# Sample attention of a decoder layer: both pages of a pair scored in one TensorE run, with two turned-page buffers and one raw-weight buffer

## The chip, the cores and the metric

The kernel runs on one core of one Trainium2 chip. The metric is the device time of one execution in microseconds (us); three executions of the kernel before were timed.

## The reference

One layer of a decoder runs for two groups that share all parameters: a prompt group (1 sequence of 2048 tokens) and a sample group (8 sequences of 4 new tokens each, with 8192 past tokens in a paged cache). What bears on the change:

```python
h = rms_norm(x, pre_g)
z = h @ w_in                     # 1024 -> 5632: ca cb cg | pu pg | q k v sg | mq mg, 512 columns each
mk, mv = split(rms_norm(mem_prompt, mem_g) @ w_mem_kv)      # 256 memory tokens, 1024 columns
# stick-breaking attention of the sample group: 8 heads x 64, 64 pages of 128 tokens per sequence
k_past = cache_k[0][page_table]; v_past = cache_v[0][page_table]
zs = q @ k^T / 8 + bias_h
beta, 1 - beta = sigmoid(zs), sigmoid(-zs)
a_j = beta_j * prod over later tokens (1 - beta)            # a suffix product over the keys
y_s = a @ v
# then: gates, concat of four branches -> w_out -> rms_norm -> residual, final rms_norm
```

All data are float32. The products with `w_in` and `w_mem_kv` are made from three products of reduced-precision parts: each weight and each activation is split into a high part and the rest (`whi`, `wlo`, `xhi`, `xlo`).

## The kernel before

TensorE's instructions stand in the order in which the program writes them; the other engines' instructions, and the DMAs on SyncE's queue (SP), are ordered by a list scheduler at build time, which works from its own estimates. Each engine then runs its list strictly in order.

**The projection stage** takes the first 1502 us. It runs over two parts of the prompt (1024 tokens each; the first part also has the 32 sample tokens) and, in each part, over 44 column blocks of `w_in` of 128 columns ("kinds": q0, q1, ..., sg3). A block is computed in column tiles of the tokens, three in the first part (384, 384 and 288 tokens) and two in the second (512 each), with 24 matmuls per tile (`mm3`, line 242). Most groups hold one block; some hold two, whose tiles alternate. While the blocks q2, q3 and k0 of the first part run, one of eight blocks of `w_mem_kv` (m0 to m7, 24 matmuls of 256 tokens) stands between each two of their tiles.

**Weights.** A block's weights arrive as one raw tile of 512 KB (`load_w`, line 226, tag `wr`, on SP's queue). ScalarE casts it to `whi` (line 232), then GpSimd subtracts to get `wlo` (line 233). There are two buffers each of `whi` and `wlo`, and `WR` raw buffers (2). `fill_w` is called whenever a block has been used up: it splits the next raw tile and orders the load of another. A raw buffer is free for its next load once GpSimd's subtraction has read it. The blocks are taken in the order of `SEQ_W`: q0, q1, q2, m0, m1, m2, q3, m3, m4, m5, k0, m6, m7, k1, k2, ...

**The sample group's attention** (`sample_stages`) is slipped in between the matmuls of this stage: a counter of projection work (`due`) lets the generator take one step about every 5 us. The eight sequences are taken four at a time; the 64 pages of such a four are taken in 32 pairs, from the last to the first, so there are 64 pairs in all. For one pair n:
- `load_k(n, ml)`, `load_v(n)`: GpSimd issues indirect DMAs (line 892): two of 1 MB for the two pages' keys (`kt`, KT = 2 buffers), four of 512 KB for the values (`vt`, VB = 4 buffers).
- `turn(n, ml)`: VectorE transposes a page of keys in 32 x 32 blocks into `T` (line 925, two instructions per page, TB = 1 buffer), then the next pair's load into the freed `kt` is ordered.
- `scores(n, ml)`: 16 matmuls of 32 stationary columns in four column groups of the array (line 938, two records each in the trace) into one PSUM bank (`sSA`).
- `weights(n)`: two sigmoids on ScalarE (`sgam`, `sbe`, lines 949 and 951), the suffix product on VectorE (a scan, line 955) and a product (line 958).
- `transposes(n)`: two full-array transposes on TensorE (line 965), copied out by ScalarE (`saT`, line 967).
- `values(n)`: 8 matmuls of 32 stationary columns and 512 moving columns (line 977, two records each).

The order per pair, with `yield` as the step to the projection matmuls:

```python
for n in range(N):
    yield
    scores(n, 0); turn(n, 1)
    yield
    if n: transposes(n - 1); yield
    scores(n, 1)
    if n: values(n - 1); load_v(n)
    weights(n)
    turn(n + 1, 0)
    yield
```

So between two stretches of projection matmuls TensorE does, in turn: one page of scores; two transposes; one page of scores and the values of the pair before. After the projection stage come the prompt's stick-breaking attention and the output projection (1502 us to the end), which share nothing with the change.

Of the kernel before, what the change touches and what calls it, by code (L numbers as in the profile page):

```python
# [8 lines left out]
F32 = mybir.dt.float32  # L9
# [9 lines left out]
P = 128  # L19
# [13 lines left out]
PART = 1024  # L33
COLS = (((0, 384), (384, 768), (768, 1056)), ((0, 512), (512, 1024)))
XW = 1056
TB = 1
SMALL = 4
K4 = 4
PACE = 4.0
# [14 lines left out]
VB = 4  # L54
# [4 lines left out]
SEND = 0.97  # L59
XA = 3  # L60
KT = 2
WR = 2


class Tasks:
# [21 lines left out]
def kernel(  # L87
# [9 lines left out]
    pe, act, dve, pool, sp = nc.tensor, nc.scalar, nc.vector, nc.gpsimd, nc.sync  # L97
# [151 lines left out]
    st = zx.enter_context(tc.tile_pool(name="st", bufs=2, side="left"))  # L249
    tasks = Tasks()  # L250

    def big(name, bufs=BIG):
        return st.tile([P, 1088], F32, tag="big", name=name, bufs=bufs)

    def small(name):
        return st.tile([P, 512], F32, tag="small", name=name, bufs=SMALL)
# [488 lines left out]
    def fill_w(n=2):  # L745

        while len(wsplit) < n and (raw or SEQ_W):
# [3 lines left out]
            wsplit[it] = split_w(raw.pop(it), "%d%s%d" % it)  # L751
        while n == 2 and len(raw) < WR and SEQ_W:
            next_raw()
# [53 lines left out]
    def sample_setup(sm, S):  # L807

        ptb = sm.tile([P, NB, NPAGE], I32, tag="T", name="ptb", bufs=TB)
        sp.dma_start(ptb.rearrange("p b n -> p (b n)"), page_table.rearrange("b n -> (b n)").partition_broadcast(P))  # L810
        io = sm.tile([P, 3], I32, name="io", bufs=1)
        pool.iota(io, pattern=[[0, 3]], base=0, channel_multiplier=1)
        iof = sm.tile([P, 3], F32, name="iof", bufs=1)
        dve.tensor_copy(iof, io)
        for c, w in ((0, 32), (1, 64)):
            for k in range(P // w):
                pr = slice(w * k, w * k + w)
                dve.tensor_scalar(out=iof[pr, c : c + 1], in0=iof[pr, c : c + 1], scalar1=-float(w * k), scalar2=None,
                                  op0=ALU.add)
        idk = sm.tile([P, 2, NPAGE], I32, name="idk", bufs=1)  # L820
        idv = sm.tile([P, NB, NPAGE // 2], I32, name="idv", bufs=1)
        for i in range(4):
            pr = slice(32 * i, 32 * i + 32)
            dve.tensor_scalar(out=idk[pr], in0=ptb[pr, i::4, :], scalar1=32.0, scalar2=iof[pr, 0:1], op0=ALU.mult,
                              op1=ALU.add)
        for k in range(2):
            pr = slice(64 * k, 64 * k + 64)
            dve.tensor_scalar(out=idv[pr], in0=ptb[pr, :, k::2], scalar1=64.0, scalar2=iof[pr, 1:2], op0=ALU.mult,
                              op1=ALU.add)
        S["idk"], S["idv"] = idk, idv  # L830

        b1 = sm.tile([P, 1], F32, name="b1", bufs=1)
        nb1 = sm.tile([P, 1], F32, name="nb1", bufs=1)
        e8 = sm.tile([P, P], F32, tag="vt", name="e8", bufs=VB)[:NH]
        bcol = sm.tile([NH, 1], F32, name="bcol", bufs=1)
        sp.dma_start(bcol, sb_bias.rearrange("o h -> h o"))
        pool.memset(e8, 0.0)
        ev = e8.rearrange("h (g x r) -> h g x r", g=4, x=2)
        pool.affine_select(out=ev, in_=ev, compare_op=ALU.not_equal, fill=1.0, base=0, pattern=[[-1, 4], [-4, 2], [0, 16]],
                           channel_multiplier=1)  # L840
        yield
        yield
        bp = tp_tile("bps")
        pe.matmul(bp[:, 0:1], lhsT=e8, rhs=bcol, start=True, stop=True)
        dve.tensor_copy(b1, bp[:, 0:1])
        dve.tensor_scalar(out=nb1, in0=b1, scalar1=-1.0, scalar2=None, op0=ALU.mult)
        S["b1"], S["nb1"] = b1, nb1

        rep = sm.tile([P, 4, 4, 32], F32, tag="vt", name="rep", bufs=VB)
        for jl in range(4):  # L850
            dve.tensor_copy(rep[:, jl], ident[:, None, 32 * jl : 32 * jl + 32].to_broadcast([P, 4, 32]))
        yield
        qps = tp_tile("qps")
        for j in range(16):
            pe.matmul(qps[:, NS * j : NS * (j + 1)], lhsT=rep[:, j % 4].rearrange("p i d -> p (i d)"),
                      rhs=qsT[:, j // 4, :], start=True, stop=True)
        qv = qps.rearrange("p (r j t) -> p r j t", r=2, j=8)
        S["W"] = []
        for k in range(2):
            W = sm.tile([P, 2, 8, 2, TS, 4], F32, name=f"W{k}", bufs=1)  # L860
            pool.memset(W, 0.0)
            for i in range(4):
                pr = slice(32 * i, 32 * i + 32)
                t0 = TS * (4 * k + i)
                for r in range(2):
                    dve.tensor_copy(W[pr, r, :, r, :, i], qv[pr, r, :, t0 : t0 + TS])
            S["W"].append(W.rearrange("p r j x q i -> p (r j) (x q i)"))

        h8 = sm.tile([P, 4, 2, 4], F32, name="h8x", bufs=1)
        pool.memset(h8, 1.0)  # L870
        pool.affine_select(out=h8, in_=h8, compare_op=ALU.is_ge, fill=0.0, base=0, pattern=[[-32, 4], [-4, 2], [-8, 4]],
                           channel_multiplier=1)
        pool.affine_select(out=h8, in_=h8, compare_op=ALU.is_ge, fill=0.0, base=3, pattern=[[32, 4], [4, 2], [8, 4]],
                           channel_multiplier=-1)
        H8 = sm.tile([P, 2, 4], F32, name="H8", bufs=1)
        dve.tensor_tensor(out=H8, in0=h8[:, 0], in1=h8[:, 1], op=ALU.add)
        for i in (2, 3):
            dve.tensor_tensor(out=H8, in0=H8, in1=h8[:, i], op=ALU.add)
        S["H8"] = H8
        S["gam"] = []  # L880
        for k in range(2):
            g = sm.tile([P, 257], F32, name=f"sgam{k}", bufs=1)
            pool.memset(g[:, 256:257], 1.0)
            S["gam"].append(g)
        S["Oc"] = con.tile([P, 2, DH], F32, name="Oc")
        yield

# [6 lines left out]
    def sample_stages(sm, sps, S):  # L894
# [25 lines left out]
        def turn(n, ml):  # L920
            if n < N:
                T = sm.tile([P, 4, 16, 32], F32, tag="T", name=f"T{n}_{ml}", bufs=TB)
                kt = kts.pop((n, ml))
                for hh in range(2):
                    dve.transpose(T[:, 2 * hh : 2 * hh + 2].rearrange("p s j t -> p (s j t)"),  # L925
                                  kt[:, 2 * hh : 2 * hh + 2].rearrange("p s j d -> p (s j d)"))
                Ts[n, ml] = T
                load_k(n + 1, ml)
# [12 lines left out]

        def weights(n):
            sS = sSs.pop(n)
            be = sm.tile([P, 256], F32, tag="sbe", name=f"sbe{n}", bufs=2)
            ga = S["gam"][n % 2]

            tok = sS[:, :256].rearrange("p (m s t) -> p m t s", m=2, s=4)
            by = dict(m=2, s=4)
            act.activation(out=ga[:, 0:256].rearrange("p (m t s) -> p m t s", **by), in_=tok, func=AF.Sigmoid,
                           bias=S["nb1"][:, 0:1], scale=-1.0)  # L950
            act.activation(out=be.rearrange("p (m t s) -> p m t s", **by), in_=tok, func=AF.Sigmoid,
                           bias=S["b1"][:, 0:1])
            E = sm.tile([P, 257], F32, tag="sE", name=f"sE{n}", bufs=2)
            prev = S.get("E") if n % NCK else None
            dve.tensor_tensor_scan(out=E[:, ::-1], data0=ga[:, ::-1], data1=zeros.to_broadcast([P, 257]),
                                   initial=1.0 if prev is None else prev[:, 0:1], op0=ALU.mult, op1=ALU.max)
            S["E"] = E
            dve.tensor_tensor(out=be, in0=be, in1=E[:, 1:257], op=ALU.mult)
            As[n] = be

        def transposes(n):
            aps = S["ps"][:, 256:512]
            bs = As.pop(n).rearrange("p (k s) -> p s k", s=2)
            for k in range(2):
                pe.transpose(aps[:, P * k : P * (k + 1)], bs[:, k, :], ident)
            aT = sm.tile([P, 2, P], F32, tag="saT", name=f"saT{n}", bufs=2)
            act.copy(aT.rearrange("p l r -> p (l r)"), aps)
            aTs[n] = aT.rearrange("p l (x i) -> p l x i", i=4)

# [21 lines left out]
        for _ in range(Y0):  # L991
            yield
        turn(0, 0)
        for n in range(N):
            yield
            scores(n, 0)
            turn(n, 1)
            yield
            if n:
                transposes(n - 1)  # L1000
                yield

            scores(n, 1)
            if n:
                values(n - 1)
                load_v(n)
            weights(n)
            turn(n + 1, 0)
            yield
        yield  # L1010
        yield
        yield
# [764 lines left out]
    S = {}  # L1777
# [222 lines left out]
    for n, x in enumerate(parts):  # L2000
# [14 lines left out]
        for k, p_ in enumerate(out_part(x) if n >= len(lead_) else lead if not n else ()):  # L2015
# [5 lines left out]
            if not n:  # L2021

                k, at_ = p_ % 4, p_ // 4
# [41 lines left out]
```

## Time and profile before

| | |
|---|---|
| median of three executions | 2429.65 us (2429.42 to 2430.13) |
| profiled execution, first to last instruction | 2426.4 us |
| TensorE busy | 2290.7 us, 94% |
| VectorE, ScalarE, GpSimd busy | 72%, 46%, 52% |
| mean granted TensorE clock | 0.982 |
| DMA | 562 MB, 231 GB/s of HBM traffic over the span |

The profile is of one execution, and its own time is its span of 2426.4 us; the timed median is 3.25 us (0.13%) above it. Lines of a timeline give start, duration, engine, line and operation, output<-input, count, and in brackets the idle time before with what ended it. "PEld" is TensorE's weight load, "SPq" the issue of a DMA by SyncE.

### The profile page before, as it was taken

To read this page: it belongs to the slowest core of one execution; us is meant where nothing else is said; L and a number is where in the kernel's file an instruction comes from. 1 tells how busy PE (TensorE), PEld (TensorE's weight loads), DVE (VectorE), ACT (ScalarE), POOL (GpSimd) and SP (SyncE) were. 2 spreads that over 40 slices of the span, in tenths; PEclk is the share of its full clock that TensorE was granted. 3 is DMA by queue.
4 is the path that set the end of the run, shared out by engine and by line. 5 is a ranking of instruction groups with operands and counts; after the bars stand their busy time and mean duration, and the time that the engine had idled before them with its cause. 6 is when DMAs were issued, how large, how long until landed. Compare 5 with 4: busy or idle time off the path is not lost. (4 is left out here: it accounts for less than half of the span.)

```text
span 2426.4 us, 42151 instructions
## 1 busy us (share of the span) xinstructions
PE 2290.7 (94%) x15962; PEld 1776.1 (73%) x15962; DVE 1736.2 (72%) x2434; ACT 1118.5 (46%) x1939; POOL 1272.7 (52%) x1309
## 2 busy tenths in 40 slices
PE   6999999999999999999999999899999998989997
PEld 6998888898887777777777776455555556777775
DVE  5332784969756665477877877888898857886898
ACT  5322343242442322124241425688989955543444
POOL 2554545556574455655555554576876844433330
PEclk9999999999999999999999999999999999999998
DMA  5678988887778799987877776834332227887764
GB/s 184 213 253 285 350 290 292 290 263 265 261 253 275 271 346 329 312 285 253 290 265 271 260 239 164 239 81 118 101 88 73 63 63 239 272 279 254 238 240 161
DMA packets 340438, 562.15 MB, mean 232 GB/s; under 512 B 28481, under 2 KB 212929, under 8 KB 323834
## 3 DMA queue, kind: packets, MB, share of 16 engines
q1 hardware_dynamic: 284858, 290.72, 39.1%
q0 software_dynamic: 55376, 268.72, 31.1%
q8 instruction: 126, 2.06, 0.3%
q14 instruction: 78, 0.64, 0.1%
HBM read 469.28 MB, written 90.68 MB: 231 GB/s over the span
## 5 line engine op out<-in xcount | busy, mean ns | idle before, releaser
L925 DVE STREAM_TRANSPOSE T<-kt 128x1024 f32<-128x1024 f32 x256 | 308.8, 1226 | 193.6 <-PE sSA L938 183.0
L892 POOL DMA_INDIRECT vt<-in_cache_v_dram,idv x256 | 250.4, 978 | 239.7 <-PE sO L977 178.8
L583 DVE SCALAR_TENSOR_TENSOR cacc<-U,par,cacc 128x512 f32<-128x512 f32 x480 | 360.1, 750 | 11.8
L1277 POOL TENSOR_TENSOR be<-be,E 128x512 f32<-128x512 f32 (+2 forms) x320 | 303.5, 956 | 117.0 <-DVE E L1268 52.6
L1268 DVE TENSOR_TENSOR_SCAN E<-gam,cr,ZM 128x513 f32<-128x513 f32 x192 | 232.9, 1262 | 14.4 <-ACT gam L1253 13.2
L892 POOL DMA_INDIRECT kt<-in_cache_k_dram,idk x128 | 125.6, 981 | 206.9 <-DVE T L925 152.5
L1288 PEld LDWEIGHTS AT<-ident,be 128*128 128x128 f32 x1088 | 117.9, 142 | 127.3 <-ACT at L1294 45.3
L1885 PE MATMUL acc<-wohi,mh 128*128 128x512 f32 (+1 forms) x480 | 193.6, 403 | 3.9 <-DVE mh L1650 2.0
L1253 ACT ACTIVATE gam<-S,nbias_bc 128x1024 f32<-128x1024 f32 (+1 forms) x160 | 172.5, 1078 | 51.2 <-ACT be L1255 18.9
L1885 PE MATMUL acc<-wolo,mh 128*128 128x512 f32 (+1 forms) x480 | 190.8, 397 | 0.0
L1885 PE MATMUL acc<-wohi,ml 128*128 128x512 f32 x448 | 179.2, 400 | 12.1 <-DVE ml L1650 12.1
L1248 PE MATMUL S<-kT,Q 128*128 128x512 f32 (+1 forms) x640 | 177.9, 401 | 6.1 <-ACT be L1255 2.6
L1288 PE MATMUL AT<-ident,be 128*128 128x128 f32 x1088 | 158.4, 284 | 13.8 <-DVE at L1292 3.9
L1255 ACT ACTIVATE be<-S,bias_bc 128x1024 f32<-128x1024 f32 (+1 forms) x160 | 171.4, 1071 | 0.0
L1304 PE MATMUL av<-at,V 128*64 128x512 f32 (+3 forms) x640 | 153.0, 557 | 1.7 <-DVE sbo L1309 1.7
L938 PE MATMUL sSA<-T,W 128*32 128x128 f32 x4096 | 140.8, 277 | 7.6 <-DVE T L925 6.4
L938 PEld LDWEIGHTS sSA<-T,W 128*32 128x32 f32 x4096 | 105.4, 110 | 44.9 <-issue 37.2
L977 PE MATMUL sO<-vt,saT 128*32 128x512 f32 x1024 | 123.7, 597 | 0.0
L1248 PEld LDWEIGHTS S<-kT,Q 128*128 128x128 f32 x640 | 107.3, 196 | 22.2 <-ACT be L1255 3.5
L1650 DVE TENSOR_TENSOR ml<-mr,mh 128x512 fp32r<-128x512 f32 x108 | 97.0, 905 | 33.6 <-ACT mh L1639 33.4
L1265 DVE TENSOR_TENSOR_SCAN E<-gam,ZM 128x128 f32<-128x128 f32 (+3 forms) x128 | 96.4, 802 | 29.3 <-ACT gam L1253 22.3
L1294 ACT COPY at<-AT 128x512 f32<-128x512 f32 x192 | 109.0, 656 | 14.4 <-PE AT L1288 14.4
(571 smaller groups left out, 6032.8 us busy)
## 6 DMA issues: line engine op xcount, KB each, us to landing
Q<-qd SPq DMA_DIRECT2D x64, 256.0 KB
mr<-mixd SPq DMA_DIRECT2D x32, 512.0 KB
mr<-mixd SPq DMA_DIRECT2D x48, 256.0 KB
wor<-in_w_out_dram SPq DMA_DIRECT2D x20, 512.0 KB
xtp<-in_x_prompt_dram SPq DMA_DIRECT2D x16, 512.0 KB
kT<-kd SPq DMA_DIRECT2D x64, 128.0 KB
wor<-in_w_out_dram SPq DMA_DIRECT2D x32, 256.0 KB
msd<-mr SPq DMA_DIRECT2D x32, 256.0 KB
```

The lines of the kernel that those rows point to most:

```text
L583: dve.scalar_tensor_tensor(out=ps, in0=U[:, a + k : a + k + H], scalar=wd[:, k : k + 1], in1=ps, op0=ALU.mult, op1=ALU.add)
L892: pool.indirect_dma_start(out=dst, out_offset=None, in_=rows, in_offset=bass.IndirectOffsetOnAxis(ap=idx, axis=0))
L925: dve.transpose(T[:, 2 * hh : 2 * hh + 2].rearrange("p s j t -> p (s j t)"), kt[:, 2 * hh : 2 * hh + 2].rearrange("p s j d -> p (s j d)"))
L938: pe.matmul(sSs[n][32 * g : 32 * g + 32, P * ml : P * (ml + 1)], lhsT=W[:, jj, :], rhs=T[:, :, jj, :], start=i == 0, stop=i == 3, tile_pos ...
L1248: pe.matmul(S[:, j, :w], lhsT=Q[hh][:, x, P * (q2 + j) : P * (q2 + j + 1)], rhs=KT[hp, hh, kc][:, :w], start=x == 0, stop=x == 1)
L1253: act.activation(out=ga[:, :, 512 - w : 512], in_=S[:, :, :w], func=AF.Sigmoid, bias=nbias_bc[:, h : h + 1], scale=-1.0)
L1255: act.activation(out=be[:, :, :w], in_=S[:, :, :w], func=AF.Sigmoid, bias=bias_bc[:, h : h + 1])
L1268: dve.tensor_tensor_scan(out=E[:, j][:, ::-1], data0=ga[:, j][:, ::-1], data1=ZM[:, 0:1].to_broadcast([P, 513]), initial=carry[hh, q2][:, ...
L1277: pool.tensor_tensor(out=be[:, j, :m], in0=be[:, j, :m], in1=E[:, j, 513 - w : 513 - w + m], op=ALU.mult)
L1288: pe.transpose(ap_[:, P * qt : P * (qt + 1)], A[hp, qb, kc, hh, qt][:, P * r : P * (r + 1)], ident)
L1304: pe.matmul(av[64 * hh : 64 * hh + 64, c], lhsT=V[:, 4 * kc + r, 64 * hh : 64 * hh + 64], rhs=ats.pop((hp, qb, kc, r, hh))[:, c], start=dg ...
L1885: pe.matmul(o[:rows], lhsT=m[a][:, k, :rows], rhs=W[prod, 4 * h + k][w], start=not cont and h == k == n == 0, stop=h == 1 and k == 3 and n ...
```

## The change

`scores(n, 0)` moves from its own step down to the step of `scores(n, 1)`, so that both pages' scores and `values(n - 1)` stand in one run on TensorE; the step that it leaves is kept as an empty one, so that a pair still takes four steps. Both pages of the next pair are turned right after that run, into two `T` buffers instead of one. `transposes(n - 1)` comes two steps after `weights(n - 1)` instead of three, and two steps ahead of `values(n - 1)` instead of one. To make room in SBUF there is one raw-weight buffer instead of two (`WR`), and one buffer instead of two for `sgam`, `sbe` and `saT`; `h8x` uses a `vt` buffer during set-up, and the tag `big` is 32 columns narrower.

```diff
-TB = 1
+TB = 2
...
-WR = 2
+WR = 1
...
-        return st.tile([P, 1088], F32, tag="big", name=name, bufs=bufs)
+        return st.tile([P, 1056], F32, tag="big", name=name, bufs=bufs)
...
-        h8 = sm.tile([P, 4, 2, 4], F32, name="h8x", bufs=1)
+        h8 = sm.tile([P, 4, 2, 4], F32, tag="vt", name="h8x", bufs=VB)
...
-            be = sm.tile([P, 256], F32, tag="sbe", name=f"sbe{n}", bufs=2)
-            ga = S["gam"][n % 2]
+            be = sm.tile([P, 256], F32, tag="sbe", name=f"sbe{n}", bufs=1)
+            ga = S["gam"][0]
...
-            aT = sm.tile([P, 2, P], F32, tag="saT", name=f"saT{n}", bufs=2)
+            aT = sm.tile([P, 2, P], F32, tag="saT", name=f"saT{n}", bufs=1)
...
         turn(0, 0)
+        turn(0, 1)
         for n in range(N):
             yield
-            scores(n, 0)
-            turn(n, 1)
             yield
             if n:
                 transposes(n - 1)
                 yield
-
+                yield
+            scores(n, 0)
             scores(n, 1)
             if n:
                 values(n - 1)
                 load_v(n)
             weights(n)
             turn(n + 1, 0)
-            yield
+            turn(n + 1, 1)
```

In the instruction order of the changed program TensorE has 63 runs of page, page, values, one of two pages, one of values and 64 of transposes, where the program before has 65 runs of a page alone, 63 of page and values, one of values and 64 of transposes; TensorE's instructions are as many as before. On SP every load of a raw weight tile from the second on stands behind a wait for GpSimd's subtraction of the tile before it.

More of the change, by code (lines that the diff above doesn't have):

```diff
@@ L880, in sample_setup @@
         S["gam"] = []
[L881 to L884, printed above, removed]
+        g = sm.tile([P, 257], F32, name="sgam", bufs=1)
+        pool.memset(g[:, 256:257], 1.0)
+        S["gam"].append(g)
         S["Oc"] = con.tile([P, 2, DH], F32, name="Oc")
```

## The prediction

> **What bounds the kernel now.** I read the page first, then busy time by stretches of the span, then TensorE's waits in the projection stage, and then timelines around single runs of the sample group.
>
> ```profile
> span 2426.4 us, 42151 instructions
> ```
>
> ```profile
> core 0: us, PE busy (x) PEld busy (x) DVE busy (x) ACT busy (x) POOL busy (x), PEclk, DMA share, GB/s
> 0.00:56.00 56.00, 35.90 (x208) 32.51 (x209) 31.15 (x49) 30.60 (x63) 10.94 (x35) 1.00 0.59 197
> 56.00:126.00 70.00, 66.12 (x477) 64.03 (x476) 25.24 (x40) 24.36 (x43) 39.24 (x27) 1.00 0.63 196
> 126.00:1502.00 1376.00, 1348.42 (x10953) 1103.24 (x10952) 927.07 (x1260) 444.49 (x832) 738.77 (x687) 0.99 0.82 278
> ```
>
> The reader is to see that TensorE sets the time of the projection stage: it is busy for 1348 of 1376 us from 126 us on, and for 66 of 70 us in the stretch before, where the memory blocks m0 to m7 run. What shortens or delays TensorE's list there moves the end one for one, since nothing after 1502 us is changed. Of the 28 us in which it is idle in the long stretch, its waits name these two that touch the change:
>
> ```profile
> engine line waited for: us in total, times, longest us
> PE sSA L938 <- DVE T L925: 6.4, 4, 3.8
> ...
> PE z0sg L242 <- POOL wlo0sg L233: 2.2, 2, 2.0
> ```
>
> **The change, part 1: the runs.** A page alone, between matmuls of a projection block, and a page followed by values (timeline of TensorE):
>
> ```profile
> 574.27 0.34 PE L242 MATMUL z0cg<-xlo,whi0cg 128*128 128x384 f32 x1
> 574.44 0.34 PE L242 MATMUL z0cg<-xhi,wlo0cg 128*128 128x384 f32 x1
> 574.71 1.08 PE L938 MATMUL sSA<-T,W 128*32 128x128 f32 x32
> 575.72 0.44 PE L242 MATMUL z0cg<-xhi,whi0cg 128*128 128x384 f32 x1
> 576.00 0.34 PE L242 MATMUL z0cg<-xlo,whi0cg 128*128 128x384 f32 x1
> ```
>
> ```profile
> 604.36 1.08 PE L938 MATMUL sSA<-T,W 128*32 128x128 f32 x32
> 605.25 1.90 PE L977 MATMUL sO<-vt,saT 128*32 128x512 f32 x16
> ```
>
> Projection matmuls start 0.17 us apart (574.27, 574.44). From 574.44 to 576.00 are 1.56 us with two such steps in them, so the page alone costs TensorE 1.56 - 2 x 0.17 = 1.22 us. In front of values it costs 605.25 - 604.36 = 0.89 us: the array goes from 128 to 32 columns and back only once for the run. Each of the 64 pairs gets one page for 0.89 instead of 1.22 us: 64 x 0.33 = 21 us, minus. This is TensorE's own time, with nothing beside it that could hide it, and I take it whole.
>
> **Part 2: two turned pages, two steps for the weights.** `T` is now turned four steps ahead of its use instead of two, so the 6.4 us of waits for it go. The price is on the other side: `transposes` come one step earlier after `weights`. The pace is in the first and last page of scores, and the slack of one pair in these rows:
>
> ```profile
> L938 PE MATMUL sSA<-T,W x4096: 269/273/423, 168.5 to 1455.7; 128*32 128x128 f32 x196
> ```
>
> ```profile
> 611.03 0.39 DVE L958 TENSOR_TENSOR sbe<-sbe,sE 128x256 f32<-128x256 f32 x1
> ```
>
> ```profile
> 618.49 0.39 PE L965 MATMUL sSA<-ident,sbe 128*128 128x128 f32 x2
> ```
>
> (1455.7 - 168.5) / 63.5 pairs = 20.3 us per pair, 5.07 us per step. The product ends at 611.42 and TensorE comes for it at 618.49, 7.1 us later; one step less leaves 2.0 us. VectorE's list has in both programs page transposes between the scan and this product, so it ends no earlier. Where VectorE is late today `T` is late; tomorrow `sbe` will be, at some pairs. Bounds: nothing, and the 6.4 us back again. I take 2.5 us. So this part is -6.4 + 2.5 = -3.9 us. The single buffers of `sgam`, `sbe` and `saT` are free long before their next writer (a pair is 20.3 us) and cost nothing; if a scan were late by a step it would be the wait above. Order on GpSimd: its queue now holds for a pair one page of keys, four of values and the other page in a row; that is a rival below.
>
> **Part 3: one raw-weight buffer.** One load in the stage of the memory blocks was waited for, and shows the whole cycle; with it, the end of q2's subtraction and the start of k1 (timelines of GpSimd, SP, ScalarE and TensorE):
>
> ```profile
> 57.28 2.40 POOL L233 TENSOR_TENSOR wlo0q<-wr0q,whi0q 128x1024 fp32r<-128x1024 f32 x1 [5.72 <-ACT whi0q L232]
> ```
>
> ```profile
> 101.17 0.37 SPq L226 DMA_DIRECT2D wr0mem<-in_w_mem_kv_dram  x1
> ...
> 109.77 0.37 SPq L226 DMA_DIRECT2D wr0k<-in_w_in_dram  x1
> ```
>
> ```profile
> 106.23 1.04 ACT L232 CAST whi0mem<-wr0mem 128x1024 fp32r<-128x1024 f32 x1 [3.92 <-DMA wr0mem<-in_w_mem_kv_dram]
> ```
>
> ```profile
> 107.36 2.39 POOL L233 TENSOR_TENSOR wlo0mem<-wr0mem,whi0mem 128x1024 fp32r<-128x1024 f32 x1 [1.74 <-ACT whi0mem L232]
> ```
>
> ```profile
> 125.73 0.42 PE L242 MATMUL z0k<-xhi,whi0k 128*128 128x384 f32 x1
> ```
>
> Load 101.17 to 106.23 = 5.06 us, cast 1.04, subtraction to 109.75, and at 109.77 SP issues the next load that waited for this buffer: 8.60 us. Today another raw tile lies ready meanwhile. With one buffer the load of each block waits for the subtraction of the block before it, and the cycle becomes the pace. From q2's subtraction (end 59.68) to k1's come 11 blocks (m0, m1, m2, q3, m3, m4, m5, k0, m6, m7, k1), and TensorE uses them up in 125.73 - 59.68 = 66.0 us, 6.0 us each. 11 x 8.60 = 94.6 us, 28.6 us more than now. TensorE's list is fixed, so it stands still meanwhile. Behind SP's wait stand stores of finished tiles, which nobody on this path awaits; the casts wait in ScalarE's list, and evacuations behind them concern tiles of which TensorE needs the next buffer only after that same cast.
>
> The load time is the unknown. Above it stands the first one of the kernel, among loads of x; below, none that was waited for:
>
> ```profile
> 1.74 0.43 SPq L226 DMA_DIRECT2D wr0q<-in_w_in_dram  x1
> ```
>
> ```profile
> 9.04 1.05 ACT L232 CAST whi0q<-wr0q 128x1024 fp32r<-128x1024 f32 x1 [2.85 <-DMA wr0q<-in_w_in_dram]
> ```
>
> That is 7.30 us, a cycle of 10.8 us, and 53 us in all; from below, a load as short as 2.5 us would make the cycle 6.0 us and hide it wholly. I take a cycle of 8.8 us, near the row of the same stage and a little over it, since some loads will share the DMA engines with stores: 11 x 8.8 - 66.0 = 30.8 us.
>
> Later in the stage a block lasts about 16 us (1376 us over some 83 blocks), against a cycle of 8.6 to 10.8, so a load is ready in time; where two blocks close within one tile of each other, the second split comes late but has a block's time to spare. Bounds: 0, and a second helping of the 2.2 us of waits for `wlo0sg`; I take 0 and leave the other to the range.
>
> At the start the second raw tile (q1) waits for the first one's subtraction, but q1 is first used after 30 us, so that is hidden. The scheduler, though, puts the third raw tile's wait ahead of the load of x tile 7, and this tile's square (ScalarE) now comes right before the copy of the first projection tile, for which TensorE waits already:
>
> ```profile
> 25.03 1.06 ACT L195 ACTIVATE sq<-xtp 128x1024 bf16<-128x1024 f32 x1 [0.47 <-DMA xtp<-in_x_prompt_dram]
> 26.00 0.19 ACT L195 ACTIVATION_READ_ACCUMULATOR sq<-xtp 128x1 f32 x1
> ...
> 26.56 0.30 ACT L198 ACTIVATE rs<-rs,eps_t 128x1 f32<-128x1 f32 x1
> ```
>
> ```profile
> PE z0q L242 <- ACT zt0q L654: 2.1, 1, 2.1
> ```
>
> 1.06 + 0.19 + 0.30 is 1.5 us more in that wait. Bounds: -1.5 (the x tiles load earlier without q1 among them) and +1.5; I take +1.5.
>
> **Sum.** -21 - 3.9 + 30.8 + 1.5 = +7.4 us on the profiled 2426.4; the timed median lies 3.25 us above that span, which I leave as it is: 2429.65 + 7.4 = 2437 us.
>
> [...] An idle stretch of TensorE, 3.6 of 9 us, was followed by this:
>
> ```profile
> 360.00:369.00 9.00, 5.37 (x34) 4.90 (x32) 2.47 (x5) 7.05 (x14) 4.47 (x5) 1.00 0.92 307
> 369.00:376.00 7.00, 6.26 (x50) 5.58 (x51) 5.60 (x11) 1.85 (x3) 1.82 (x2) 0.51 0.56 230
> ```
>
> For 7 us TensorE had half its clock, which costs 3.5 us if it has work for all of them. The new waits are uneven, as the starts of a memory block, of the next projection tile and of the next memory block show:
>
> ```profile
> 109.98 0.28 PE L242 MATMUL mz<-mhi,whi0mem 128*128 128x256 f32 x1
> ...
> 112.97 0.42 PE L242 MATMUL z0k<-xhi,whi0k 128*128 128x384 f32 x1
> ...
> 117.47 0.28 PE L242 MATMUL mz<-mhi,whi0mem 128*128 128x256 f32 x1
> ```
>
> A cycle that covers a memory block alone (3.0 us of matmuls) leaves over 5 us idle, one that covers a projection tile alone (4.5 us) 4 us, one that covers both about 1 us; five of the eleven are of the long kinds. [...]
>
> **The rivals.** (1) The half clock is not absorbed: five spells of 3.5 us add 17 us, 2455 us. For it: the row above. Against: short waits of about 1 us stand in every second cycle but the chain of loads does not lengthen. Chance 0.15.
> (2) Faster: the load cycle is short. Alone in flight, a load has the DMA engines (busy 0.63 of the stretch) more to itself than in the row above. It decides at 8.1 us per cycle, where 11 x 8.1 - 66.0 = 23 us are what parts 1, 2 and the start bring in (-23.4). At 7.4 us (a load of 3.9 us) it is 15.4 us and the kernel takes 2422 us; wholly hidden, 2406 us. Against it stands the only load that was waited for. Chance 0.20.
> (3) The burst: all six indirect loads of a pair are now ordered together.
>
> ```profile
> q0 software_dynamic: 55376, 268.72, 31.1%
> ```
>
> ```profile
> L892 POOL DMA_INDIRECT vt<-in_cache_v_dram,idv x256 | 250.4, 978 | 239.7 <-PE sO L977 178.8
> ```
>
> 31.1% of 2426.4 over 64 pairs is 11.8 us of all engines per pair, and of the six issues at 0.98 us the last page of keys is the sixth. With the other queue's share (0.82 in all) the burst takes some 15 us of the pair's 20.3, so it fits with 2 to 5 us to spare. If it doesn't at the closest quarter of the pairs, VectorE stands before `T` and evacuations wait behind it: 16 x 1.5 = 24 us, 2461 us. Chance 0.10.
> That the runs are not merged is excluded by the instruction order.
>
> **How the numbers follow.** The forecast has 0.55: a cycle of 8.6 to 9.2 us and the bounds of parts 2 and 3 give 2428 to 2446 us. About 0.2% (4.9 us) is what a measurement of this kernel can tell from no change. Of the forecast's 0.55 I put 0.16 within it and 0.39 slower; rivals 1 and 3 are slower (0.23, with 0.02 within); of rival 2, 0.17 faster and 0.03 within. Faster 0.17, same 0.21, slower 0.62. For 8 in 10 the range goes from rival 2's 7.4 us cycle, a little under it, 2416, to between rivals 1 and 3, 2458 us.
>
> **What would show it.** Right: in the profile after, TensorE's busy time in the stretch from 56 us to the start of k1 spread over some 95 us instead of 66, with waits for `wlo0mem`, `wlo0q`, `wlo0k` summing to about 30 us; casts of the memory blocks 8.6 to 9 us apart and idle before them for the raw tile's DMA; a run of two pages and values near 0.89 + 0.89 + 2 us; no wait for `T` on TensorE. Wrong: casts under 8 us apart, waits for `sbe` of over 5 us in sum, a clock far under 0.98, or VectorE idle before `T` for the keys' DMA.

## The result: 2.4% slower

The changed kernel takes 2488.31 us (median of 4 executions, 2483.63 to 2489.99), the kernel before on the same chip 2429.53 us: a ratio of 1.0238, with a 95% interval of 1.022 to 1.0257, or 58.8 us more. The prediction was 2437 us with a range to 2458. The profiled execution after has a time of 2487.31 us and this span:

```profile
span 2485.6 us, 42065 instructions
```

That is 59.2 us above the span before. Stretches of the span (columns as in the prediction's: length, busy time of TensorE, of its weight loads, of VectorE, ScalarE and GpSimd, clock, DMA share, GB/s); the second one goes from the end of q2's subtraction to k1's first matmul, the third to the first matmul of the prompt's attention:

```profile
63.11:154.15 91.04, 71.84 (x449) 67.35 (x448) 23.96 (x40) 21.94 (x39) 36.09 (x27) 0.91 0.47 147
154.15:1562.16 1408.01, 1342.11 (x10956) 1122.48 (x10953) 931.89 (x1261) 441.22 (x829) 747.40 (x687) 0.98 0.78 272
1562.16:2485.60 923.44, 841.24 (x4328) 576.02 (x4328) 754.01 (x1085) 619.29 (x1002) 487.93 (x560) 0.96 0.56 168
```

The same two stretches of the kernel before:

```profile
59.68:125.73 66.05, 62.17 (x448) 60.34 (x448) 22.78 (x40) 22.57 (x40) 36.57 (x27) 1.00 0.66 205
125.73:1502.77 1377.04, 1348.69 (x10956) 1103.51 (x10953) 928.03 (x1261) 444.54 (x832) 739.81 (x689) 0.99 0.82 278
```

The start is 3.4 us longer (63.11 against 59.68), the stage of the memory blocks 25.0 us, the steady part of the projection stage (the third stretch above) 31.0 us; what follows is unchanged (923.4 against 923.6). The second number is the load chain that was predicted. The third was predicted as a gain of 25 us. In that part TensorE is busy 6.6 us less, although its clock is lower (0.98 against 0.99), and idle 65.9 us instead of 28.4.

**The chain of loads.** Issues of the raw tiles on SP, and GpSimd's first and last subtraction of the chain:

```profile
63.14 0.40 SPq L226 DMA_DIRECT2D wr0mem<-in_w_mem_kv_dram  x1
...
71.03 0.39 SPq L226 DMA_DIRECT2D wr0mem<-in_w_mem_kv_dram  x1
...
80.03 0.38 SPq L226 DMA_DIRECT2D wr0mem<-in_w_mem_kv_dram  x1
...
88.37 0.37 SPq L226 DMA_DIRECT2D wr0q<-in_w_in_dram  x1
...
60.71 2.40 POOL L233 TENSOR_TENSOR wlo0q<-wr0q,whi0q 128x1024 fp32r<-128x1024 f32 x1 [5.73 <-ACT whi0q L232]
...
150.68 2.38 POOL L233 TENSOR_TENSOR wlo0k<-wr0k,whi0k 128x1024 fp32r<-128x1024 f32 x1 [3.83 <-ACT whi0k L232]
```

Each load is issued once the subtraction before it has ended: 11 cycles in 153.06 - 63.11 = 89.95 us, 8.18 us each, and 1.1 us more to k1's first matmul at 154.15.

**The merged run.** The timeline of TensorE, with lines one lower than before:

```profile
680.53 1.95 PE L937 MATMUL sSA<-T,W 128*32 128x128 f32 x64
682.30 1.90 PE L976 MATMUL sO<-vt,saT 128*32 128x512 f32 x16
684.13 0.45 PE L242 MATMUL z0sg<-xhi,whi0sg 128*128 128x384 f32 x1
```

Two pages take 682.30 - 680.53 = 1.77 us, 2 x 0.89. Less the projection's own steps, the medians over all runs are 3.80 us for page, page, values, and before 1.21 for a page plus 2.93 for page and values: 0.34 us less per pair, 21.8 us for 64. The wait for `T` is gone as well (the group of all scores, its last column the idle time before them):

```profile
L937 PE MATMUL sSA<-T,W 128*32 128x128 f32 x4096 | 126.0, 275 | 0.0
```

**The new waits.** TensorE's waits in the steady part:

```profile
PE z0cb L242 <- ACT us_s L692: 13.5, 1, 13.5
PE z0sg L242 <- POOL wlo0sg L233: 6.6, 2, 4.6
PE qps L855 <- DVE b L845: 5.4, 1, 5.4
PE ms L475 <- DVE pL L517: 5.1, 1, 5.1
PE trcs L613 <- POOL tcs L792: 4.3, 1, 4.3
```

No single one is the loss: they are many, on GpSimd, VectorE and ScalarE, and most concern tiles that the change doesn't touch. The largest begins on SP:

```profile
276.66 11.04 SPq L273 DMA_DIRECT2D xs<-in_x_prompt_dram  x3
287.79 0.39 SPq L226 DMA_DIRECT2D wr0pu<-in_w_in_dram  x1
```

```profile
304.15 1.04 ACT L232 CAST whi0pu<-wr0pu 128x1024 fp32r<-128x1024 f32 x1 [18.91 <-DMA wr0pu<-in_w_in_dram]
305.11 0.37 ACT L690 COPY U<-z0ca 128x256 f32<-128x256 f32 x1
305.37 0.19 ACT L692 COPY us_s<-z0ca 128x32 f32<-128x32 f32 x1
```

```profile
297.00:311.00 14.00, 5.39 (x18) 5.29 (x19) 0.00 (x0) 2.17 (x5) 3.19 (x2) 0.51 0.37 141
```

Three loads of x rows, one of them after a wait of 7.0 us, stand ahead of the load of `wr0pu` on SP and hold it back for 11.1 us (276.66 to 287.79). The load itself then takes until its cast at 304.15, 16.4 us against 5.06 us in the prediction's row; the six gathers of a pair go out beside it (GpSimd's timeline), but how much of the 16.4 us is theirs is not shown:

```profile
286.18 1.13 POOL L891 DMA_INDIRECT kt<-in_cache_k_dram,idk  x1 [7.88 <-DVE T L924]
...
292.60 0.94 POOL L891 DMA_INDIRECT kt<-in_cache_k_dram,idk  x1 [0.30 <-issue]
```

The cast waits for 18.9 us at the head of ScalarE's list, and behind it wait the copies that free the accumulator of the last `ca` tile. TensorE stands 13.5 us for those, and the clock is at half from 297.15 to 310.80 us. The late raw tile thus also held up evacuations (those copies at 305.11 and 305.37), which the prediction excluded ("TensorE needs the next buffer only after that same cast").

**The clock.** By the trace's clock records TensorE was at half speed for 68.3 us of the steady part in 10 spells, against 23.9 us in 4 before. It was busy for 52.1 and 22.4 us of them, and half of that is lost: 26.1 and 11.2 us. So the 31.0 us are 37.5 us of idle time and 14.9 us of half clock more, and 21.5 us less of TensorE's own work at full clock.

### The profile page after: what moved, and what is told of

The parts are those of the page before. It is cut to its first block, busy times and chain, and to the rows that moved or that the text cites. A ratio compares the mean times of both kernels' runs of the same rounds, so it can differ in the third digit from the quotient of the medians.

```text
span 2485.6 us, 42065 instructions
## 1 busy us (share of the span) xinstructions
PE 2295.2 (92%) x15962; PEld 1803.0 (73%) x15962; DVE 1745.2 (70%) x2434; ACT 1114.9 (45%) x1935; POOL 1284.5 (52%) x1308
## 5 line engine op out<-in xcount | busy, mean ns | idle before, releaser
L937 PE MATMUL sSA<-T,W 128*32 128x128 f32 x4096 | 126.0, 275 | 0.0
L1247 PEld LDWEIGHTS S<-kT,Q 128*128 128x128 f32 x640 | 106.9, 195 | 22.4 <-issue 4.7
L937 PEld LDWEIGHTS sSA<-T,W 128*32 128x32 f32 x4096 | 108.7, 110 | 18.9 <-issue 15.4
```

Source lines behind the costliest of these rows:

```text
L937: pe.matmul(sSs[n][32 * g : 32 * g + 32, P * ml : P * (ml + 1)], lhsT=W[:, jj, :], rhs=T[:, :, jj, :], start=i == 0, stop=i == 3, tile_pos ...
L1247: pe.matmul(S[:, j, :w], lhsT=Q[hh][:, x, P * (q2 + j) : P * (q2 + j + 1)], rhs=KT[hp, hh, kc][:, :w], start=x == 0, stop=x == 1)
```

## The experiments

The theory after the result: the one raw buffer costs the time (A), in the stage of the memory blocks and, through late loads, later too. The rival (B): later, the cost is in the new order of the sample group, which bunches work on other engines after each run. A ratio is always to the kernel before, timed beside the run on the same chip.

**e1: only the raw buffer.** The kernel before with

```diff
-WR = 2
+WR = 1
```

> The kernel before with one raw-weight buffer (WR = 1) and nothing else of the change. Theory A (the one raw buffer costs the time, in the stage of the memory blocks and later in the stage too): k1's first matmul starts about 28 us later than before, the rest of the projection stage grows by about 53 us in waits and half clock, and no run is merged, so the time is 2429.5 + 28 + 53 = about 2510 us (2495 to 2520). Theory B (the one raw buffer costs only the memory-block stage; what is lost later comes from the new order of the sample group, with its six gathers in a row): 2429.5 + 28 = about 2458 us (2452 to 2465), the steady stage as before.

Ratio 1.0163 (1.0141 to 1.0185). Its stretches from 59 us on:

```profile
59.00:153.45 94.45, 75.28 (x474) 70.37 (x472) 27.54 (x40) 23.11 (x41) 38.41 (x27) 0.91 0.45 142
153.45:1532.87 1379.42, 1348.46 (x10956) 1105.48 (x10954) 930.04 (x1261) 445.02 (x833) 742.36 (x688) 0.99 0.81 278
```

k1 starts at 153.45 us, 27.7 later than before; the steady part is 2.4 us longer. Theory A falls for the steady part: with the old order one raw buffer costs little there. (The medians differ by 37.5 us, the two spans by 31.0; the spans are from different chips, and the 6.5 us between are not placed. If all of them lay in the steady part, it would be 8.9 us.)

**e2 and e3: only the order.** The changed kernel with `WR = 2`, room made by `K4 = 3`; and the kernel before with `K4 = 3`.

> The changed kernel with two raw-weight buffers again; room for it is made by K4 = 3 (one 4 KB buffer less for x rows and other short-lived tiles; the next run has the same cut in the kernel before). Theory A: the merge's 22 us and the waits for T are left as gains, about 2405 us (2400 to 2412) plus what the K4 cut costs. Theory B: the memory-block stage is as before, the steady stage keeps its 31 us net loss, about 2461 us.

> The kernel before with K4 = 3, as a measure for the cut in the run above. Both theories: within 5 us of the kernel before; if not, the difference is taken off the run above.

1.0102 (1.0078 to 1.0125) and 1.005 (1.0033 to 1.0067). The cut isn't free (e3 was expected within 5 us of the kernel before and is 12 us above it), but beside it the new order is some 0.5% slower, not 22 us faster. So the changed kernel's loss doesn't end with the raw buffer. e2's median, 2443.12 us, lies between its two theories and meets neither.

**e4 and e8: the raw tile in halves.** One raw tile's memory as two tiles of 2 KB, each with its own load, cast and subtraction, in the changed kernel (e4) and in the kernel before (e8):

```diff
-        raw_ = wp.tile([P, ND, P], F32, tag="wr", name="wr%d%s%d" % it, bufs=WR)
-        wq.dma_start(raw_, src[:, o : o + P].rearrange("(d p) n -> p d n", p=P))
+        v = src[:, o : o + P].rearrange("(d p) n -> p d n", p=P)
+        raw_ = []
+        for h in range(2):
+            raw_.append(wp.tile([P, ND // 2, P], F32, tag="wr", name="wr%d%s%d" % it + f"h{h}", bufs=2))
+            wq.dma_start(raw_[h], v[:, 4 * h : 4 * h + 4])
...
-        act.copy(hi, raw)
-        pool.tensor_tensor(out=lo, in0=raw, in1=hi.bitcast(F32), op=ALU.subtract)
+        for h in range(2):
+            hh = hi[:, 4 * h : 4 * h + 4]
+            act.copy(hh, raw[h])
+            pool.tensor_tensor(out=lo[:, 4 * h : 4 * h + 4], in0=raw[h], in1=hh.bitcast(F32), op=ALU.subtract)
```

> The changed kernel with the one raw buffer of 4 KB as two of 2 KB: each block's weights come as two loads of 256 KB, each with its own cast and subtraction, so that one half loads while the other is split; no memory is added. Theory A: the cycle of a half is a load of 3 to 4 us, 0.55 us cast and 1.2 us subtraction, about 5.3 us with both halves overlapping, under the 6.0 us of a memory block: most of the 28 us goes and most of the waits later, 2405 to 2425 us. Theory B: the memory-block stage as before, the steady stage's loss stays, about 2461 us.

> The kernel before with the raw tile as two of 2 KB (one raw tile's memory in all), nothing else of the change: the measure for the halves alone. Stage of the memory blocks as in e4, 5 to 7 us longer than before; the rest as before: 2427 to 2432 us beside 2421 to 2430 of the kernel before. The difference of e4 to it is what the new order of the sample group costs or brings by itself.

1.0093 (1.0063 to 1.0123) and 1.0065 (1.0043 to 1.0088). In e4 k1 starts at 132.85 us instead of 154.15: the chain of loads was the cost of that stage. The median of e4, 2439.4 us, lies between its two theories. e8 missed its expectation: halves cost 0.65% by themselves. That the order is slower can't be told from this pair.

**e5, e6, e7: the bunch spread, on e4.** In e5 `turn(n + 1, 1)` moves one step later, in e6 `load_v(n)`, in e7 `load_v` one step and the second turn two (the diff is e7's):

```diff
             if n:
                 values(n - 1)
-                load_v(n)
             weights(n)
             turn(n + 1, 0)
-            turn(n + 1, 1)
...
         for n in range(N):
             yield
+            if n > 1:
+                load_v(n - 1)
             yield
             if n:
+                turn(n, 1)
                 transposes(n - 1)
```

> The changed kernel with the raw tile in halves (as e4), and the second page of the next pair turned one step (5 us) later, so that VectorE turns one page at a time and its gather comes a step after the other five. Theory A (the list of GpSimd: six gathers in a row, near 7.6 us, stand ahead of the subtraction that makes wlo): five of six are still in a row, so it gains little on e4: 0 to 5 us, about 2435 us on the first chip's scale. Theory B (VectorE: two pages of keys turned in a row, 4.8 us, hold up what stands behind them): most of e4's new waits go, 12 to 18 us better than e4, about 2424 us.

> As e4, with the four gathers of values ordered one step later than the run that frees their buffers, both pages still turned together. Theory A: gathers come as two and four, no longer six: most of the waits for wlo go (some 8 us with their half clock 12), about 2427 us. Theory B: VectorE's two pages in a row stay, no gain on e4: about 2439 us.

> As e4, with the gathers of values one step later and the second page turned two steps later. Both theories: e4's new waits go; the merged runs' 22 us are left over the kernel before less what the halves cost: 2405 to 2420 us, faster than the kernel before. If it stays near e4 (2439 us), the loss is neither GpSimd's list nor VectorE's two pages, but the load of the merged runs on something else, as the short time between the weights and the transposes.

1.0098 (1.0065 to 1.0131), 1.0245 (1.0203 to 1.0288), 1.0147 (1.0112 to 1.0182). e5 brought nothing; e6 and e7 missed both theories. The group of the values' matmuls, in e4 and then in e6 (last column: idle time before, and for what):

```profile
L981 PE MATMUL sO<-vt,saT 128*32 128x512 f32 x1024 | 123.5, 593 | 0.0
```

```profile
L981 PE MATMUL sO<-vt,saT 128*32 128x512 f32 x1024 | 166.3, 598 | 19.3 <-DMA vt<-in_cache_v_dram,idv 19.2
```

With three steps (15 us) instead of four for the gathers of values, TensorE waits for them: 19.3 us ahead of the matmuls, and the matmuls themselves are counted busy 42.8 us longer. Nothing can be read from e6 and e7 about the bunch. So in e12 each gather keeps its whole pair of time (20.3 us).

**e9: the late load at 305 us.** The changed kernel with a delay ahead of the loads of x rows, so that `wr0pu` stands before them on SP:

```diff
 WR = 1
+STATS_LATE = 32
...
     def later_stats():
 
+        for _ in range(STATS_LATE):
+            yield
```

> The changed kernel (one raw buffer) with the loads of x rows for the later statistics (xs) ordered 32 steps later, so that none stands ahead of the load wr0pu on SP's queue. Theory A (what the one raw buffer and the new order cost together beyond their single costs is the one wait of 13.5 us at 305 us, with 6.8 us of half clock after it): 20 us less than the changed kernel, a ratio of about 1.0155 to the kernel before. Theory B (a late load somewhere is the rule with one buffer, and only its place moves): within 6 us of the changed kernel, a ratio of 1.021 to 1.026.

1.0201 (1.0184 to 1.0218): the wait of 13.5 us is gone, but 9 of the expected 20 us are saved; another wait, 9.7 us of the memory attention's scores for a softmax row at 405 us (the same matmul waits 5.1 us, for VectorE's `pL`, in the changed kernel, at 421 us), has taken part of its place. That lies between the two expectations.

**e10 and e11: the order again, with a free cut.** The changed kernel with `WR = 2`, `BIG = 4`; the kernel before with `BIG = 4`.

> The changed kernel with two raw buffers, the room made by BIG = 4 (one 4.2 KB buffer less for finished tiles of the projection) instead of K4 = 3. Against the next run it gives the new order's net effect without the raw buffer, a second time: as in e2 against e3, 5 to 15 us slower than the next run (the merge's 22 us gained, some 30 us lost). If the loss in e2 came from the K4 cut meeting the new order, it is faster than the next run by 10 to 25 us instead.

> The kernel before with BIG = 4, as measure for the cut in the runs beside it: 0 to 15 us slower than the kernel before under every theory.

1.0055 (1.0039 to 1.0072) and 1.0008 (0.9992 to 1.0023). This cut costs nothing that can be told, so the new order by itself costs about 0.5% (0.55%, or 0.47% against e11), 11 to 14 us. The steady part, e11 then e10:

```profile
125.15:1500.35 1375.20, 1346.89 (x10956) 1103.89 (x10954) 933.00 (x1261) 444.87 (x832) 743.75 (x689) 0.99 0.82 278
```

```profile
127.97:1522.24 1394.27, 1342.21 (x10956) 1119.55 (x10953) 925.19 (x1261) 439.29 (x828) 747.70 (x688) 0.98 0.79 274
```

Of +19.1 us, idle time is +23.7 (52.06 against 28.31) and half clock +14.0 (half of the time that TensorE is busy in the spells, 48.4 against 20.5 us); the rest, TensorE's own work at full clock, is -18.6. So the merge brings about what was predicted, and the waits with their half clock take it and more. (e10's profiled execution was its longest, 2453.81 us with a median of 2439.6, so its waits may be above the usual; e2's, of 2440.25, has 55.06 us of idle time in the same stretch.) In e11 TensorE waits 2.3 us for `wlo0sg` and 0.7 us for `wlo0pg`. Its waits for GpSimd's list in e10, and how one of them comes about:

```profile
PE z0sg L242 <- POOL wlo0sg L233: 9.0, 3, 6.1
...
PE z0pg L242 <- POOL wlo0pg L233: 3.0, 1, 3.0
PE z0mq L242 <- POOL wlo0mq L233: 3.0, 1, 3.0
```

```profile
774.80 1.18 POOL L891 DMA_INDIRECT kt<-in_cache_k_dram,idk  x1 [5.54 <-DVE T L924]
776.28 1.14 POOL L891 DMA_INDIRECT vt<-in_cache_v_dram,idv  x1 [0.30 <-issue]
...
781.46 0.94 POOL L891 DMA_INDIRECT kt<-in_cache_k_dram,idk  x1 [0.30 <-issue]
782.42 0.65 POOL L698 TENSOR_TENSOR U<-U,sg0cb 128x256 f32<-128x256 f32 x1
783.01 0.26 POOL L701 TENSOR_TENSOR us_s<-us_s,sg0cb 128x32 f32<-128x32 f32 x1
783.23 2.34 POOL L233 TENSOR_TENSOR wlo0sg<-wr0sg,whi0sg 128x1024 fp32r<-128x1024 f32 x1
```

The cast of this block ended at 775.77. Six gathers, from 774.80 to 782.42, stand ahead of its subtraction, and TensorE waits 6.1 us for `wlo0sg`; from 782 to 789 us TensorE's clock is 0.53. Here GpSimd had itself stood 5.5 us for VectorE's turning of the page.

**e12: every gather with its whole pair of time.** On e10: after a run the weights come first; the pages are turned one and two steps later, each with its gather behind it.

```diff
         for n in range(N):
             yield
-            yield
             if n:
+                turn(n, 0)
+            yield
+            if n:
+                turn(n, 1)
                 transposes(n - 1)
...
             weights(n)
-            turn(n + 1, 0)
-            turn(n + 1, 1)
```

> As e10 (two raw buffers, BIG = 4, merged runs, two T), but after a run VectorE does the weights first, and the two pages of the next pair are turned one and two steps later, each with its gather behind it; the gathers of values stay where they are, so that each gather has a whole pair of time. Theory A (the bunch after the run, six gathers on GpSimd and two pages on VectorE, makes what stands behind it late): 15 to 25 us less than e10, a ratio below 1 if BIG = 4 costs nothing. Theory B (the loss is in the merged run itself or in the early transposes): as e10, within 5 us.

1.0043 (1.0027 to 1.006), not to be told from e10: theory B of this run, that the bunch isn't the cause, seems to hold. The longest waits, on both lists still:

```profile
PE ms L475 <- DVE pL L517: 8.5, 1, 8.5
PE z0sg L242 <- POOL wlo0sg L233: 6.4, 3, 3.6
PE ms L475 <- DVE mh0mq L712: 4.0, 1, 4.0
PE z0pg L242 <- POOL wlo0pg L233: 3.5, 1, 3.5
```

**e13, e14, e15: GpSimd's list relieved.** The subtraction of twelve blocks on VectorE, in the merged order (e10), the spread one (e12) and the order before (e11):

```diff
-        pool.tensor_tensor(out=lo, in0=raw, in1=hi.bitcast(F32), op=ALU.subtract)
+        eng = dve if nm[:-1] in ("0pg", "0mq", "0sg") else pool
+        eng.tensor_tensor(out=lo, in0=raw, in1=hi.bitcast(F32), op=ALU.subtract)
```

> e10 (merged runs, two raw buffers, BIG = 4) with the subtraction that makes wlo on VectorE for the twelve blocks pg, mq and sg of the first part, all other blocks on GpSimd as before. Theory A (GpSimd's list with the gathers makes the loss): e10's waits for wlo, 15 us, go, and with them up to 10 us of half clock: 15 to 25 us less than e10, a ratio of 0.995 to 0.999 to the kernel before. Theory B (VectorE's list, fuller after each run, makes it): 12 x some 1.2 us more on VectorE at the places where it is late, the waits stay or turn into waits for VectorE: no less than e10, a ratio of 1.004 to 1.010.

> e12 (the two pages turned one and two steps after the run) with the same twelve subtractions on VectorE. Theory A: e12's waits for wlo, 11 us, go with their half clock: 10 to 18 us less than e12, a ratio of 0.996 to 1.000. Theory B: as e12, a ratio of 1.002 to 1.008.

> e11 (the kernel before with BIG = 4) with the same twelve subtractions on VectorE, as measure: it has 3 us of waits for wlo to lose. Theory A: 0 to 5 us less than e11. Theory B: up to 10 us more.

1.005 (1.0033 to 1.0067), 0.9978 (0.9964 to 0.9992) and 1.0005 (0.9989 to 1.0022). e13 came out within theory B's range, e14 within theory A's. In e13 the waits for `wlo` of pg, mq and sg are gone but for 0.5 us, and others stand in their place:

```profile
PE my L502 <- ACT pT L517: 7.2, 2, 4.0
PE ms L476 <- DVE mh0mq L713: 6.5, 2, 3.3
PE ms L476 <- DVE mh1mq L713: 4.1, 3, 2.2
```

The longest for `mh0mq` comes at 488.40 us, out of VectorE's list (without the conv steps and the weights between them):

```profile
483.10 1.23 DVE L925 STREAM_TRANSPOSE T<-kt 128x1024 f32<-128x1024 f32 x1
...
484.89 1.23 DVE L925 STREAM_TRANSPOSE T<-kt 128x1024 f32<-128x1024 f32 x1
...
486.67 1.23 DVE L925 STREAM_TRANSPOSE T<-kt 128x1024 f32<-128x1024 f32 x1
487.83 0.52 DVE L713 SCALAR_TENSOR_TENSOR mh0mq<-z0mq,mh0mq 128x384 fp32r<-128x384 f32 x1
```

The two turned pages (four instructions) stand ahead of it. In e14, where they come a step apart and GpSimd is relieved too, both together bring what neither did alone by its ratio:

```profile
128.43:1496.02 1367.59, 1332.62 (x10957) 1114.68 (x10954) 929.35 (x1273) 439.95 (x828) 722.70 (x676) 0.99 0.81 280
```

Idle time is 35.0 us instead of e10's 52.1; e12 has 46.6 and e13 42.4, so in these single executions each relief takes a part, and e10's was its longest. e14 is the fastest kernel here, 0.22% ahead of the kernel before (0.08 to 0.36). It keeps the merged runs, the two `T`, the early transposes and the single buffers of `sgam`, `sbe` and `saT`, with two raw buffers, so none of these is the loss by itself. Of the merge's 21 us it keeps 5 by its ratio: against e11 its own work is 21.6 us less, but idle time is 6.7 us and half clock 7.3 us more. e15 shows that the old order gains nothing by the same relief.

## Why the prediction was right or wrong

| step | predicted, us | measured, us |
|---|---|---|
| merged runs | -21 | -21.8 by the runs' medians (own work -21.5; -18.6 in e10 against e11) |
| waits for `T` / for `sbe` | -6.4 / +2.5 | gone / none named |
| chain of 11 loads | +30.8 | +25.0 (cycle 8.18, not 8.8; 1.1 behind the last) |
| start | +1.5 | +3.4 |
| raw buffer later in the stage | 0 | +2.4 alone (e1; 8.9 at most); with the new order a wait of 13.5 |
| new waits by the new order | 0 | +23.7 (e10 against e11) |
| half clock after them | 0 | +14.0 (e10 against e11) |

**Right: the gain of the merge.** Two pages in front of values cost 0.89 us each, and TensorE's own work fell by 21.5 us.

**Right: the raw buffer.** The mechanism and place were right; start and chain together were put at 32.3 us, the profile has k1 28.4 us later and e1, with nothing but this edit, 27.7. The cycle was a little shorter than the row it was taken from. The mark of about 30 us of waits for `wlo` was wrong: in the stretch TensorE is idle 19.2 us, and its clock is 0.91. Since each load waits for the subtraction before it, and not for TensorE, the half clock there (17.1 us) may have filled part of the wait; no run tests this by itself.

**Wrong: what the early turns do to the other engines.** The step that failed is the end of parts 1 and 2: the 21 us were taken "whole" as the kernel's gain, and the sum held no price for six gathers in a row on GpSimd and four transposes in a row on VectorE. It named the queue and left it to rival 3, at 0.10 and 24 us, as a matter of the DMA engines: VectorE standing before `T`. That the size was near is luck, for the place was another: VectorE's wait for the keys' DMA rose only from 6.6 to 12.3 us. What became late is what stands behind the bunch in the two lists: `wlo` behind the gathers (15.0 us of TensorE's waits in e10 for pg, mq and sg), and `mh0mq` or `pL` behind the turned pages. Spreading the pages left waits on both lists (e12), relieving GpSimd's left them on VectorE's and ScalarE's (e13), and both together brought the time back under the kernel before (e14). So the row of the waits before, 28 us of idle time with 2.2 us for `wlo0sg`, should have been read as a balance of several lists that are all nearly late, not as slack.

**Wrong with the new order: "a load is ready in time" later in the stage.** Part 3 set a cycle of 8.6 to 10.8 us against some 16 us per block. That held with the old order: in e1 the load of `wr0pu` goes out at 276.68 us, its cast begins at 289.4, and TensorE doesn't wait. In the changed kernel the load was held on SP for 11.1 us and then took 16.4 us itself, about as long as a block lasts, and TensorE waited 13.5 us.

**Wrong: half clock only in the memory stage.** Rival 1 priced it at five spells there. No run shows that each long wait of that stage brings a spell; the changed kernel has three there (3.4, 6.8 and 6.8 us, 17.1 us in sum, 7.5 us of them lost by the count above), and they did not make the chain of loads longer than predicted. Those that cost came in the steady part, where no chain of loads takes them up. In e10 the clock was 0.53 from 782 to 789 us, at the wait of 6.1 us for `wlo0sg`, and 0.50 for 3.4 us behind a wait of 2.25 us (1386.07 to 1388.32); in all, the 23.7 us of new waits came with 14.0 us lost to half clock.

**How the parts add up.** By ratios: 1.63% for the raw buffer, 0.55% for the order, 2.38% for both. The 0.2% between, 5 us, is no more than the intervals leave open. The wait at 305 us is in the changed kernel and not in e1, e2 or e10, so it takes both; taking it away returned 0.37% (e9). What caused each of the remaining small waits of the new order (an x row's DMA, `pT` behind table loads on ScalarE, 1.28 us for the one at 740.13 in e10) was not taken apart. And since the scheduler writes the lists of the other engines anew for every program, no run moves one instruction alone: that the bunch on two lists makes the loss rests on the four ratios of e10, e12, e13 and e14 and on single waits followed through, not on an edit of nothing else.

## What to carry to other kernels

A gain on the engine that sets the pace arrives only if the engines that feed it can follow; here 18.6 us of TensorE's own work went against 37.7 us of new waits and half clock (e10). When an edit moves work of one step into a burst, list what stands behind that burst in each engine's list and who awaits it, and give the later list a price of its own. Where several lists are nearly late, relieving one may show next to nothing (ratios of 1.0043 in e12 and 1.005 in e13, against 1.0055 in e10); try two together before dropping the idea (0.9978 in e14). Price a buffer that is taken away where its use is densest: one raw tile cost 28 us where a block takes 6 us, and with the old order 2.4 us over the blocks of 16 us (e1).

## What the runs showed of the hardware

In e10, TensorE stood for 2.25 us, from 1386.07 to 1388.32, and worked before and after (a line of its timeline, then two stretches):

```profile
1388.32 0.74 PE L475 MATMUL ms<-mkT,mh1mq 128*128 128x256 f32 x4 [2.25 <-DVE mh1mq L712]
```

```profile
1384.00:1389.40 5.40, 3.15 (x19) 2.54 (x19) 5.26 (x9) 1.59 (x4) 5.06 (x5) 1.00 1.03 375
1389.40:1392.80 3.40, 3.40 (x10) 2.62 (x9) 3.37 (x7) 1.02 (x4) 0.56 (x2) 0.50 0.94 336
```

A spell of 3.4 us at half speed followed.

In the steady parts before and after, the 14 spells of half clock last from 3.4 to 13.7 us. How long TensorE stood did not by itself tell whether one would follow: in the changed kernel it stood for 1.93 us, from 69.14 to 71.06 (and 1.33 us up to 68.63), and the clock was at half from 71.87 to 75.28; it stood for 2.14 us, from 542.07 to 544.21, and the clock stayed full until 631 us. In the kernel before, half clock from 147.16 to 153.99 us came while TensorE was busy throughout, with 1.09 us of idle time ahead of `qps` at 144.40 as its longest wait in the 8 us before. What brought it there is open.

One gather takes GpSimd 1.30 us from issue to issue in e10's rows (776.28 to 781.46 in four steps), so that six of them hold its list for 7.6 us (774.80 to 782.42). And gathers of 2 MB of values that were ordered 15 us ahead of their use came late: TensorE stood 19.3 us for them in all (e6).
